# Weight blocks of the feed-forward projections as whole tiles loaded one set ahead, sums written in place

## The chip, the core and the metric

The kernel runs on one core of a Trainium2 chip. The metric is the device time of one execution in microseconds (us). The engines are TensorE (PE; PEld is its weight load), VectorE (DVE), ScalarE (ACT), GpSimd (POOL) and SyncE (SP), whose queue issues most of the transfers.

## The reference, cut to what matters

One encoder layer is computed for 512 + 16 new tokens of one stream and 64 of a running one: attention in two head groups, an output projection, then a gated feed-forward network of width 5632 and a last norm. The change lies in the feed-forward part:

```python
D_MODEL = 2048
D_FF = ((8 * D_MODEL // 3 + 255) // 256) * 256      # 5632
...
    h = rmsnorm(x, lp['norm_ffn_g'])
    x = x + (jax.nn.silu(h @ lp['ffn_w_gate']) * (h @ lp['ffn_w_up'])) @ lp['ffn_w_down']
...
y_prompt = rmsnorm(xp[:, N_META:], final_norm_g)
y_sample = rmsnorm(xs, final_norm_g)
```

All is float32; 576 tokens reach this part (64 and 512).

## The kernel before

**Precision.** A float32 product is made of fp32r products. `split` (L155) makes a high part `wh` on ACT (L156) and the rest `wl` = source - `wh` on DVE (L153). A tile of weights meets the tokens in three matmuls: `wh` with the tokens' high and low parts (L1219), `wl` with the high part (L1223).

**Seven products.** Gate and up take 256 columns at a time, over all 2048 rows. Such a block is seen as eight groups of 2x2 corners of 128x128 (`a11`, `a12`, `a21`, `a22`), and the tokens are cut in two halves of 288, so that seven products of corner sums do for eight (`winograd`, L1154). Left factors by number of the product: 1 is `a11`, 2 is `a12`, 4 is `a22`; 5 is `a21 + a22`, 6 is that less `a11`, 3 is `a12` less the factor of 6, 7 is `a11 - a21`. They run in the order 1, 2, 4, 5, 6, 3, 7 (`WIDE`), in the down projection 1, 5, 6, 2, 7, 3, 4 (`CHAIN`). I call the seven products of one block a set: 7 products of 24 matmuls (16 with `wh`, then 8 with `wl`), 168 in all. There are 44 sets, gate and up in turn (22 pairs, `u` in L1379); the first runs in two halves.

**Factors.** The sums are new tiles `ws`, three buffers (`subtotal`, L1174): 5 and 7 on POOL, 6 and 3 on DVE. `wh` and `wl` have two buffers each, so a product can be split once the one two places earlier is multiplied.

**Raw blocks.** A block is loaded as two halves of 8 K-tiles (1 MB each, L1387). Three buffers of a half take turns, two in the pool `fr`, one in `rw`. A buffer is free when the sums that read it (on POOL and DVE) and the splits are done.

**After a set.** `combined` (L1287) takes the products out of PSUM: copies on ACT (1, 4, 5, 6; L1296) and additions on DVE (2, 3 and twice 7; L1299). `gated` (L1355) multiplies gate by the norm on DVE, applies Silu on ACT, multiplies on POOL (L1360). After the up set POOL multiplies the two (L1420, two halves) and forms four differences of quarters (L1425 to L1428). Then `spill_operands` (L1336) splits the eight quarters: a copy on ACT (L1341), a subtraction on DVE that is written over the quarter (L1342), two stores per four quarters. It is a generator; `step` (L1397) advances it after products, after the fifth in a gate set and after each in an up set. The tiles `c` of gate and up have two buffers each.

**Down.** Five blocks of four such groups and a plain one of two; each block runs over 8 pairs of column tiles `d`, 84 matmuls each (12 a product) in the first five. Its weights come in blocks of 1 MB (`fetch_raw`, two buffers in `fr`), the operands from the spill (`builder`, L1323), the residual `y` from `x2spill` (`load_y`, L1369). The first sum of the first block is made ahead (`total`, L1433). At the end `finish` (L1487) turns the result around on TensorE and writes it out through four buffers `ot`.

**What sets the order.** PE runs as written. The other engines' queues and SP's are filled by a scheduler that follows the program's order but moves instructions up; within its queue each engine runs strictly in order.

Of the kernel before, what the change touches and what calls it, by code (L numbers as in the profile page):

```python
# [11 lines left out]
F32 = mybir.dt.float32  # L12
# [7 lines left out]
P = 128  # L20
D = 2048
KC = D // P
# [93 lines left out]
def encoder_step(  # L116
# [22 lines left out]
    def store(dst, src):  # L139
        nc.sync.dma_start(dst, src)  # L140
# [1012 lines left out]

    def winograd(wpool, spool, raws, slots, take, banks=None, engine=V, step=lambda: None, stag=("ws", 3),  # L1154
                 chain=(), total=None):

# [16 lines left out]

        def subtotal(n, engine, op, xs, ys):  # L1174

            w = spool.tile([P, n, P], F32, name="ws", tag=stag[0], bufs=stag[1])
            k = 0
            for i in range(max(len(xs), len(ys))):
                m = min(x[i].shape[1] for x in (xs, ys) if len(x) > i)
                pick = lambda z: z[i] if len(z) > i and z[i].shape[1] == m else z[0][:, k:k + m, :]  # L1180
                engine.tensor_tensor(w[:, k:k + m, :], pick(xs), pick(ys), op=op)  # L1181
                k += m
            return w
# [4 lines left out]
        sums = {}  # L1188

        def lhs(p):  # L1190
            if p == 5 and total is not None:
                sums[1] = total
                return split_weights(n, [total])
            if p == 6 and total is not None:
                sums[2] = total
                engine.tensor_tensor(total, total, a11[0], op=ALU.subtract)
                return split_weights(n, [total])
            if p in (1, 2, 4):
                return split_weights(n, {1: a11, 2: a12, 4: a22}[p])
# [8 lines left out]
            return split_weights(n, [s])  # L1208

# [37 lines left out]
    for i in range(KC):  # L1247
# [23 lines left out]
        if i == 2:  # L1271
            raw0 = load_raw(rw, w_gate, 0, 8, 0, 1)

    close_mx()
    fr, close_fr = pool("fr")
    fw, close_fw = pool("fw")
    banks0 = {}
# [3 lines left out]
    fb, close_fb = pool("fb", "right")  # L1281

# [53 lines left out]
    def spill_operands(m, parts):  # L1336

        for first, src in parts:
            hi = squad(F32R)
            for k in range(4):  # L1340
                S.activation(hi[:, k], src[:, k], AF.Copy)  # L1341
                V.tensor_tensor(src[:, k].bitcast(F32R), src[:, k], f32(hi[:, k]), op=ALU.subtract)  # L1342
                yield
            store(opspill[m, :, first:first + 4, 0], f32(hi))
            store(opspill[m, :, first:first + 4, 1], src)

    def token_norm():
# [21 lines left out]
    def load_y(d):  # L1369
        if d < 4:  # L1370
            y2 = fc.tile([P, 2, TQ], F32, name="y", tag="c" + "ggu"[d // 2 * 2], bufs=2)
        else:
            y2 = yy.tile([P, 2, TQ], F32, name=f"y{d}")
        for f in range(2):
            y[2 * d + f] = y2[:, f]
            load(y2[:, f], x2spill[2 * d + f])

    start = builder(0, blocks[0], False, True)
    for u in range(FC // 2):  # L1379
        out = {}  # L1380
        for which, wsrc in (("g", w_gate), ("u", w_up)):
            first = turn == 0
            raws = []
            for hf in range(2):
                if turn:
                    rp, bufs = (rw, 1) if turn % 3 == 0 else (fr, 2)
                    raws.append(load_raw(rp, wsrc, hf * 1024, 8, u * 256, bufs))  # L1387
                turn += 1
            c = fc.tile([P, 2, TQ], F32, name="c", tag="c" + which, bufs=2)
            chain = () if first else CHAIN if u == FC // 2 - 1 and which == "u" else WIDE  # L1390
            take = combined(*quarters(c[:, 0, :], c[:, 1, :]), chain)
            if u == FC // 2 - 1 and which == "u":
                raw_down = load_raw(fr, w_down, 0, 2 * blocks[0], 0, 2, start=G.dma_start)
# [15 lines left out]
            if first:  # L1409
                winograd(fw, fb, raws, range(4, 8), take, banks0, step=step)  # L1410
            else:
                winograd(fw, fb, raws, range(8), take, step=step, chain=chain)
            out[which] = c
# [18 lines left out]
        spilling = spill_operands(u, parts)  # L1432
    total = squad()[:, :, 0:P]  # L1433
    corners = raw_down.rearrange("p (m t) (f c) -> p t f m c", t=2, f=2)[:, :, 1]
    G.tensor_tensor(total, corners[:, 0], corners[:, 1], op=ALU.add)
    close_fb()
    close_rw()
    yy, close_yy = pool("yy", "right")

# [20 lines left out]
    def down_rows(m0, n, d, slots, step):  # L1460
# [8 lines left out]
        winograd(fw, yy, raws, slots, take, step=step, chain=CHAIN,  # L1469
                 total=None if m0 + d else total)  # L1470

# [15 lines left out]
    def finish(h, ahead):  # L1487
# [48 lines left out]
    sizes = dict(zip(np.cumsum([0] + blocks).tolist(), blocks))  # L1536
    fetched = {wanted.pop(0): raw_down}

    def fetch_raw():
        if wanted:  # L1540
            key = wanted.pop(0)
            fetched[key] = load_raw(fr, w_down, key[0] * 256, 2 * sizes[key[0]], key[1] * 256, 2)

    for _ in start:
        pass
    first = 0
    for bi, n in enumerate(blocks):
        slots = [(first + k) % 8 for k in range(n)]
        if bi + 1 < len(blocks):
            build = builder(first + n, blocks[bi + 1], bi + 2 == len(blocks))  # L1550

            def step():
                if bi or d:
                    next(spilling, None)
                    next(build, None)

            for d in range(KC // 2):
                fetch_raw()
                if bi == 0 and d + 1 < KC // 2:
                    load_y(d + 1)  # L1560
                down_rows(first, n, d, slots, step)
            for _ in build:
                pass
        else:
            before = iter(())
            for h in range(2):
                for d in range(KC // 2):
                    fetch_raw()
                    plain_rows(first, n, d, (h,), slots, squares)
# [7 lines left out]
    close_yy()  # L1577
    close_fc()
    close_fw()
# [70 lines left out]
```

## Time and profile before

| | |
|---|---|
| median of 3 runs | 2533.42 us (2527.93 to 2533.64) |
| the profiled execution | 2525.37 us, of which the span is 2523.5 us |
| PE busy | 2408.5 us, 95%, 17544 matmuls |
| DVE, ACT, POOL busy | 1851.3, 1138.6 and 822.8 us |
| gate and up sets | 916.57 to 1983.30 us of the span |
| down projection, blocks of four | 1983.30 to 2439.5 us |
| transfers | 271.68 MB read, 81.16 MB written |

Busy time contains the time in which an instruction has begun but waits inside the engine, so a POOL or DVE instruction that stands beside another can be longer than alone. A row of the timeline gives start, length, engine, line, operation and tiles, and in brackets the idle time of the engine before it with what ended it.

### The profile page before, as it was taken

The numbers are of one execution on the slowest core, as the hardware profiler recorded it, in microseconds if no ns is written. First come the engines' busy times: TensorE is split into PE (matmuls) and PEld (weight loads), VectorE is DVE, ScalarE is ACT, GpSimd is POOL, SyncE is SP. The second block draws the span as 40 slices with busy tenths as digits, with TensorE's granted clock in tenths as the row PEclk, the third lists the DMA queues.
The fourth block names the chain that finished last, engine by engine and source line by source line (L and its number), as shares of the span: only waits on it lengthen the run. The fifth ranks groups of instructions, "written<-read, shape, count | busy, mean of one in ns | idle before, by whom it ended". The sixth has DMA issues, their size and how long they took to land. (4 is left out here: it accounts for less than half of the span.)

```text
span 2523.5 us, 44543 instructions
## 1 busy us (share of the span) xinstructions
PE 2408.5 (95%) x17544; PEld 2352.1 (93%) x17544; DVE 1851.3 (73%) x2963; ACT 1138.6 (45%) x2091; POOL 822.8 (33%) x625
## 2 busy tenths in 40 slices
PE   8999999999999999999999999999999999999997
PEld 7999999999998888999998998999999999999997
DVE  5666766577664677777777777777877888898875
ACT  5454544334443444444444444444444433333345
POOL 1100000120001655454455455455455322222236
PEclk9999999999999999999999999999999999999999
DMA  7433233252335543444444435344445874654434
GB/s 225 137 91 89 82 97 90 72 166 86 88 96 158 149 136 105 138 141 139 138 133 148 130 126 160 108 138 141 140 138 164 295 268 157 228 179 137 137 94 151
DMA packets 362742, 353.06 MB, mean 140 GB/s; under 512 B 25086, under 2 KB 320660, under 8 KB 362532
## 3 DMA queue, kind: packets, MB, share of 16 engines
q1 hardware_dynamic: 360575, 344.48, 43.1%
q0 software_dynamic: 1632, 5.19, 0.7%
q8 instruction: 138, 2.26, 0.4%
q10 hardware_dynamic: 325, 0.53, 0.1%
q14 instruction: 72, 0.59, 0.1%
HBM read 271.68 MB, written 81.16 MB: 140 GB/s over the span
## 5 line engine op out<-in xcount | busy, mean ns | idle before, releaser
L1219 PE MATMUL m<-b,wh 128*128 128x288 f32 x7168 | 1054.5, 296 | 3.4 <-ACT wh L156 3.3
L1219 PEld LDWEIGHTS m<-b,wh 128*128 128x128 f32 x7168 | 990.2, 190 | 6.5 <-ACT wh L156 5.2
L1223 PE MATMUL m<-b,wl 128*128 128x288 f32 x3584 | 593.7, 301 | 54.4 <-DVE wl L153 52.6
L1181 POOL TENSOR_TENSOR ws<-raw 128x512 f32<-128x512 f32 x255 | 417.7, 1650 | 584.8 <-DVE wl L153 252.4
L1223 PEld LDWEIGHTS m<-b,wl 128*128 128x128 f32 x3584 | 515.7, 190 | 71.9 <-DVE wl L153 69.4
L156 ACT ACTIVATE wh<-ws 128x512 fp32r<-128x512 f32 (+1 forms) x338 | 286.8, 849 | 351.9 <-PE m L1219 187.3
L153 DVE TENSOR_TENSOR wl<-raw,wh 128x512 fp32r<-128x512 f32 x416 | 407.7, 996 | 21.4 <-ACT wh L156 20.9
L153 DVE TENSOR_TENSOR wl<-ws,wh 128x512 fp32r<-128x512 f32 (+1 forms) x338 | 389.9, 1155 | 41.0 <-ACT wh L156 39.3
L156 ACT ACTIVATE wh<-raw 128x512 fp32r<-128x512 f32 x416 | 249.2, 624 | 214.2 <-PE m L1219 167.1
L108 PE MATMUL ps<-xh,wh 128*128 128x296 f32 x992 | 225.7, 309 | 0.0
L108 PE MATMUL ps<-xl,wh 128*128 128x296 f32 x992 | 217.6, 301 | 0.3 <-DVE xl L161 0.3
L108 PE MATMUL ps<-xh,wl 128*128 128x296 f32 x992 | 217.1, 300 | 0.0
L1181 DVE TENSOR_TENSOR ws<-ws,raw 128x512 f32<-128x512 f32 x127 | 92.2, 727 | 166.8 <-POOL ws L1181 163.4
L108 PEld LDWEIGHTS ps<-xh,wh 128*128 128x128 f32 x992 | 161.3, 190 | 3.5 <-issue 0.6
L108 PEld LDWEIGHTS ps<-xl,wh 128*128 128x128 f32 x992 | 162.2, 190 | 1.0 <-DVE xl L161 0.9
L108 PEld LDWEIGHTS ps<-xh,wl 128*128 128x128 f32 x992 | 162.2, 190 | 0.0
L1467 DVE TENSOR_TENSOR y<-y,m 128x288 f32<-128x288 f32 x280 | 125.7, 449 | 41.6 <-PE m L1223 41.5
L153 DVE TENSOR_TENSOR wl<-wr,wh 128x1024 fp32r<-128x1024 f32 (+1 forms) x110 | 121.6, 1106 | 33.1 <-ACT wh L156 31.1
L156 ACT ACTIVATE wh<-wr 128x1024 fp32r<-128x1024 f32 (+1 forms) x110 | 101.6, 927 | 68.2 <-PE ps L108 50.6
L1341 ACT ACTIVATE s<-c 128x288 fp32r<-128x288 f32 x168 | 63.1, 435 | 150.6 <-POOL c L1420 126.0
L1342 DVE TENSOR_TENSOR c<-c,s 128x288 fp32r<-128x288 f32 x168 | 90.3, 584 | 43.6 <-POOL c L1428 29.4
L1360 POOL TENSOR_TENSOR c<-c,rb 128x576 f32<-128x576 f32 x44 | 71.2, 1618 | 155.7 <-ACT c L1359 155.7
(376 smaller groups left out, 3075.6 us busy)
## 6 DMA issues: line engine op xcount, KB each, us to landing
raw<-in_ffn_w_gate SPq DMA_DIRECT2D x44, 1024.0 KB, 5.4
raw<-in_ffn_w_up SPq DMA_DIRECT2D x44, 1024.0 KB, 5.6
b<-opspill SPq DMA_DIRECT2D x148, 288.0 KB, 6.0
raw<-in_ffn_w_down SPq DMA_DIRECT2D x39, 1024.0 KB, 5.7
wr<-in_w_in SPq DMA_DIRECT2D x56, 512.0 KB, 4.1
opspill<-s SPq DMA_DIRECT2D x42, 576.0 KB, 3.2
opspill<-c SPq DMA_DIRECT2D x42, 576.0 KB, 4.8
wr<-in_w_out SPq DMA_DIRECT2D x16, 512.0 KB, 4.3
```

The costliest lines, as they stand in the source:

```text
L108: self.tc.keep_in_program_order(self.pe.matmul(out, lhsT, rhs, start=start, stop=stop))
L153: V.tensor_tensor(lo, src, f32(hi), op=ALU.subtract)
L156: S.activation(hi, src, AF.Copy)
L1181: engine.tensor_tensor(w[:, k:k + m, :], pick(xs), pick(ys), op=op)
L1219: PE.matmul(banks[p], wh[:, k, :], x, start=first and new and k == 0 and x is hi, stop=False, skip_group_check=not new)
L1223: PE.matmul(banks[p], wl[:, k, :], hi, start=False, stop=last and k == n - 1, skip_group_check=not new)
L1341: S.activation(hi[:, k], src[:, k], AF.Copy)
L1342: V.tensor_tensor(src[:, k].bitcast(F32R), src[:, k], f32(hi[:, k]), op=ALU.subtract)
L1360: G.tensor_tensor(g[:, f, :], g[:, f, :], rb2, op=ALU.mult)
L1467: V.tensor_tensor(c, c, banks[p], op=ALU.add)
```

## The change

Gate and up blocks become one tile of 16 K-tiles (2 MB), one buffer in `fr` and one in `fb`, used in turn; the block of the next set is asked for at the start of a set, ahead of its seven products (`load_pair`). A sum or difference has no tile of its own any more but for one `ws` buffer: 5 is put there by POOL, 6 is written over it by DVE, 3 over `a12` by DVE, 7 over `a21` by POOL. Where there were two instructions of 128x512 per sum and per raw split there is one of 128x1024. `step` advances the spills after products two to six in a gate set (and each in an up set); up's `c` has one buffer. In down, the first two weight blocks come in one tile of `fr` by two POOL-issued loads, the others through two buffers in the place of `fb` (`fd`), asked for after a `d` and not before; seven of the residual tiles lie in the place of the raw block; `total` is gone; the last outputs share three buffers and not four.

```diff
+        sums = []
         def lhs(p):
...
             if p == 5:
-                s = sums[1] = subtotal(n, G, ALU.add, a21, a22)
+                w = spool.tile([P, n, P], F32, name="ws", tag=stag[0], bufs=stag[1])
...
+                for x, y, z in zip(sums, a21, a22):
+                    G.tensor_tensor(x, y, z, op=ALU.add)
             elif p == 6:
-                s = sums[2] = subtotal(n, engine, ALU.subtract, [sums[1]], a11)
+                for x, y in zip(sums, a11):
+                    engine.tensor_tensor(x, x, y, op=ALU.subtract)
             elif p == 3:
-                s = subtotal(n, V, ALU.subtract, a12, [sums[2]])
-            else:
-                s = subtotal(n, G, ALU.subtract, a11, a21)
+                for x, y in zip(sums, a12):
+                    V.tensor_tensor(y, y, x, op=ALU.subtract)
+            elif p == 7:
+                for x, y in zip(a11, a21):
+                    G.tensor_tensor(y, x, y, op=ALU.subtract)
...
+    def load_pair(pool, src, c0, first=0):
+        r = pool.tile([P, 16, 256], F32, name="raw", tag="raw", bufs=1)
+        for i in range(2 - first):
+            r0 = (first + i) * 1024
+            load(r[:, 8 * i:8 * i + 8], src[r0:r0 + 1024, c0:c0 + 256].rearrange("(k p) c -> p k c", p=P))
+        return r
...
-            raws = []
-            for hf in range(2):
-                if turn:
-                    rp, bufs = (rw, 1) if turn % 3 == 0 else (fr, 2)
-                    raws.append(load_raw(rp, wsrc, hf * 1024, 8, u * 256, bufs))
-                turn += 1
-            c = fc.tile([P, 2, TQ], F32, name="c", tag="c" + which, bufs=2)
+            now = raw[:, 0:8] if first else raw
+            if turn < FC - 1:
+                raw = load_pair((fr, fb)[(turn + 1) % 2], (w_up, w_gate)[turn % 2], (turn + 1) // 2 * 256)
+            turn += 1
+            c = fc.tile([P, 2, TQ], F32, name="c", tag="c" + which, bufs=1 + (which == "g"))
...
-                if which == "u" or products[0] > 4:
+                if which == "u" or 1 < products[0] < 7:
                     next(spilling, None)
...
-            tag, bufs = ("ws", 3) if i % 4 < 3 else ("ot", 1)
+            tag, bufs = ("ws", 2) if i % 3 < 2 else ("ot", 1)
...
-                fetch_raw()
                 if bi == 0 and d + 1 < KC // 2:
                     load_y(d + 1)
                 down_rows(first, n, d, slots, step)
+                fetch_raw()
```

**SP's queue in one pair of sets, in the middle of gate and up.** Before (the spill stores are L140, the loads L137):

```order
L140 DMA opspill<-s 128x4x288
L140 DMA opspill<-c 128x4x288
L140 DMA opspill<-s 128x4x288
L137 DMA raw<-in_ffn_w_up 128x8x256
L140 DMA opspill<-c 128x4x288
L137 DMA raw<-in_ffn_w_gate 128x8x256 x2
L137 DMA raw<-in_ffn_w_up 128x8x256
```

Now:

```order
L140 DMA opspill<-s 128x4x288
L140 DMA opspill<-c 128x4x288
L140 DMA opspill<-s 128x4x288
L140 DMA opspill<-c 128x4x288
L137 DMA raw<-in_ffn_w_gate 128x8x256 x2
L137 DMA raw<-in_ffn_w_up 128x8x256 x2
```

The second half of up's block stood between the stores of the spills; both halves now stand ahead of them, behind the gate block of the same pair.

**POOL's queue, one pair.** It starts with the first sums after the multiplications of gate by the norm. Before:

```order
L1360 TENSOR_TENSOR c<-c,rb_9346 128x576 x2
L1181 TENSOR_TENSOR ws<-raw 128x512 x4
L1420 TENSOR_TENSOR c<-c 128x576
L1425 TENSOR_TENSOR c<-c 128x288
L1420 TENSOR_TENSOR c<-c 128x576
L1426 TENSOR_TENSOR c<-c 128x288
L1428 TENSOR_TENSOR c<-c 128x288
L1427 TENSOR_TENSOR c<-c 128x288
L1181 TENSOR_TENSOR ws<-raw 128x512 x4
```

Now (L1185 is the sum of product 5, L1194 the difference of product 7; the other lines moved up by three or up by one):

```order
L1357 TENSOR_TENSOR c<-c,rb_9346 128x576 x2
L1185 TENSOR_TENSOR ws<-raw 128x1024
L1194 TENSOR_TENSOR raw<-raw 128x8x128
L1421 TENSOR_TENSOR c<-c 128x576
L1426 TENSOR_TENSOR c<-c 128x288
L1421 TENSOR_TENSOR c<-c 128x576
L1427 TENSOR_TENSOR c<-c 128x288
L1429 TENSOR_TENSOR c<-c 128x288
L1428 TENSOR_TENSOR c<-c 128x288
L1185 TENSOR_TENSOR ws<-raw 128x1024
L1194 TENSOR_TENSOR raw<-raw 128x8x128
```

Four instructions became two of twice the width, at the same two places between the multiplications; the pair ahead of the two multiplications L1421 belongs to the gate set that follows.

**DVE's queue where an up set ends and the next gate set begins.** Before, from the splits of up's last products to that of product 4 of the gate set:

```order
L1181 TENSOR_TENSOR ws<-ws,raw 128x512 x2
L153 TENSOR_TENSOR wl<-ws,wh 128x1024
L1181 TENSOR_TENSOR ws<-raw,ws 128x512 x2
L1299 TENSOR_TENSOR c<-c,m 128x288
L153 TENSOR_TENSOR wl<-raw,wh 128x512 x2
L1342 TENSOR_TENSOR c<-c,s 128x288
L1299 TENSOR_TENSOR c<-c,m 128x288 x2
L153 TENSOR_TENSOR wl<-raw,wh 128x512 x2
L1342 TENSOR_TENSOR c<-c,s 128x288 x3
L153 TENSOR_TENSOR wl<-raw,wh 128x512 x2
```

Now (L1188 and L1191 are the differences of products 6 and 3):

```order
L153 TENSOR_TENSOR wl<-ws,wh 128x1024
L1188 TENSOR_TENSOR ws<-ws,raw 128x1024
L1191 TENSOR_TENSOR raw<-raw,ws 128x8x128
L153 TENSOR_TENSOR wl<-ws,wh 128x1024
L153 TENSOR_TENSOR wl<-raw,wh 128x1024 x2
L1295 TENSOR_TENSOR c<-c,m 128x288
L153 TENSOR_TENSOR wl<-raw,wh 128x1024
L1338 TENSOR_TENSOR c<-c,s 128x288
L1295 TENSOR_TENSOR c<-c,m 128x288 x2
L153 TENSOR_TENSOR wl<-raw,wh 128x1024
L1338 TENSOR_TENSOR c<-c,s 128x288 x3
L153 TENSOR_TENSOR wl<-raw,wh 128x1024
```

Before, the differences L1181 next to the split of product 7 were those of the following set, made from its block ahead of time; now a set's differences stand in the set itself, between the splits of its products 5 and 6, and no following block is touched before the split of product 7.

More of the change, by code (lines that the diff above doesn't have):

```diff
@@ L1152, in pmt, with winograd @@
         return pm.tile([P, 512], F32, name="m", tag="m")
-    def winograd(wpool, spool, raws, slots, take, banks=None, engine=V, step=lambda: None, stag=("ws", 3),
-                 chain=(), total=None):
+    def winograd(wpool, spool, raws, slots, take, banks=None, engine=V, step=lambda: None, stag=("ws", 1),
+                 chain=()):
         first, last = not banks, take is not None
@@ L1172, in split_weights @@
             return wh, wl
[L1174 to L1183, printed above, removed]
         vs = [r.rearrange("p (m t) (f c) -> p t f m c", t=2, f=2) for r in raws]
@@ L1187, in winograd @@
         a11, a12, a21, a22 = ([v[:, t, f] for v in vs] for f in range(2) for t in range(2))
-        sums = {}
+        sums = []
         def lhs(p):
[L1191 to L1199, printed above, removed]
-            if p == 5:
-                s = sums[1] = subtotal(n, G, ALU.add, a21, a22)
+            if p == 5:
+                w = spool.tile([P, n, P], F32, name="ws", tag=stag[0], bufs=stag[1])
+                ends = np.cumsum([0] + [x.shape[1] for x in a21]).tolist()
+                sums.extend(w[:, a:b, :] for a, b in zip(ends, ends[1:]))
+                for x, y, z in zip(sums, a21, a22):
+                    G.tensor_tensor(x, y, z, op=ALU.add)
             elif p == 6:
-                s = sums[2] = subtotal(n, engine, ALU.subtract, [sums[1]], a11)
+                for x, y in zip(sums, a11):
+                    engine.tensor_tensor(x, x, y, op=ALU.subtract)
             elif p == 3:
-                s = subtotal(n, V, ALU.subtract, a12, [sums[2]])
-            else:
-                s = subtotal(n, G, ALU.subtract, a11, a21)
-            return split_weights(n, [s])
+                for x, y in zip(sums, a12):
[3 more added lines that the diff above has]
+                    G.tensor_tensor(y, x, y, op=ALU.subtract)
+            return split_weights(n, {1: a11, 2: a12, 4: a22, 5: sums, 6: sums, 3: a12, 7: a21}[p])
         shared = {}
@@ L1369, in load_y @@
     def load_y(d):
[L1370 to L1376, printed above, removed]
+        if d < 3:
+            y2 = fc.tile([P, 2, TQ], F32, name="y", tag="cu" if d == 2 else "cg", bufs=1 + (d < 2))
+            y[2 * d], y[2 * d + 1] = y2[:, 0], y2[:, 1]
+        elif d == 3:
+            y7 = fr.tile([P, 7, TQ], F32, name="y7", tag="raw", bufs=1)
+            y.update((6 + i, y7[:, i]) for i in range(7))
+        if d == 6:
+            y.update((i, yy.tile([P, TQ], F32, name=f"y{i}")) for i in range(13, KC))
+        for i in (2 * d, 2 * d + 1):
+            load(y[i], x2spill[i])
     start = builder(0, blocks[0], False, True)
@@ L1392, in encoder_step @@
             if u == FC // 2 - 1 and which == "u":
-                raw_down = load_raw(fr, w_down, 0, 2 * blocks[0], 0, 2, start=G.dma_start)
+                raw = fr.tile([P, 16, 256], F32, name="raw", tag="raw", bufs=1)
+                fetched = {(0, d): raw[:, 8 * d:8 * d + 8] for d in range(2)}
+                for d in range(2):
+                    G.dma_start(fetched[0, d], w_down[0:1024, d * 256:d * 256 + 256].rearrange("(k p) c -> p k c", p=P))
             products = [0]
@@ L1409, in encoder_step @@
             if first:
-                winograd(fw, fb, raws, range(4, 8), take, banks0, step=step)
+                winograd(fw, rw, [now], range(4, 8), take, banks0, step=step)
             else:
-                winograd(fw, fb, raws, range(8), take, step=step, chain=chain)
+                winograd(fw, rw, [now], range(8), take, step=step, chain=chain)
             out[which] = c
@@ L1467, in take @@
                 V.tensor_tensor(c, c, banks[p], op=ALU.add)
-        winograd(fw, yy, raws, slots, take, step=step, chain=CHAIN,
-                 total=None if m0 + d else total)
+        spool, bufs = (yy, 2) if m0 + d else (rw, 1)
+        winograd(fw, spool, raws, slots, take, step=step, stag=("ws", bufs), chain=CHAIN)
     tok = [[(0, NS), (NS, P), (192, 96)], [(QH, P), (416, P), (544, 32)]]
@@ L1561, in encoder_step @@
                 down_rows(first, n, d, slots, step)
+                fetch_raw()
+                if bi + d == 0:
+                    for _ in spilling:
+                        pass
+                    close_rw()
+                    yy, close_yy = pool("yy", "right")
             for _ in build:
@@ L1577, in encoder_step @@
     close_yy()
+    close_fd()
     close_fc()
```

20 lines of the change are left out of this document (9 added, 11 removed).

## The prediction

> **What bounds the kernel now.** First the page, then its stretches by window, because an average over the span hides which stage waits.
>
> ```profile
> span 2523.5 us, 44543 instructions
> PE 2408.5 (95%) x17544; PEld 2352.1 (93%) x17544; DVE 1851.3 (73%) x2963; ACT 1138.6 (45%) x2091; POOL 822.8 (33%) x625
> ```
>
> The next rows are windows: the first four gate and up sets, the 38 that follow, the last two, then the down blocks; last a stretch in which TensorE never waits. The columns are the length, then busy time and count of PE, PEld, DVE, ACT and POOL, and the granted clock.
>
> ```profile
> 916.57:1020.91 104.34, 96.17 (x677) 93.45 (x678) 84.81 (x106) 47.44 (x81) 51.32 (x34) 0.97 0.37 117
> 1020.91:1937.96 917.05, 871.82 (x6385) 860.24 (x6384) 692.84 (x875) 416.63 (x722) 470.96 (x304) 0.99 0.42 137
> 1937.96:1983.30 45.34, 45.27 (x339) 44.80 (x337) 34.41 (x41) 20.35 (x33) 22.27 (x14) 1.00 0.69 229
> 1983.30:2440.00 456.70, 453.10 (x3366) 447.44 (x3365) 398.75 (x644) 178.72 (x285) 106.25 (x79) 1.00 0.55 186
> 1150.00:1200.00 50.00, 49.92 (x375) 49.69 (x375) 40.53 (x50) 24.45 (x41) 24.23 (x18) 1.00 0.40 132
> ```
>
> The last row gives the floor: 50 us for 375 matmuls, 0.1333 us each, 22.4 us for a set of 168. The 38 sets hold 6384 matmuls, 851.2 us at that rate, and take 917.05: 65.9 us are lost, 3.5 per pair (48.27 for a floor of 44.8). The first four sets lose 14.7 of 104.34 us. The down row has 456.70 us for 3366 matmuls, 448.8 at the floor, so little is to be had there. PE busy at 95% says nothing of this: the loss is in the gate and up stage.
>
> What ends TensorE's waits in the 38 sets, from the groups by shape in that window:
>
> ```profile
> L1223 PE MATMUL m<-b,wl 128*128 128x288 f32 x2129 | 338.7, 301 | 45.2 <-DVE wl L153 45.0
> ```
>
> So 45 of the 65.9 us are waits for the low part of a split. Most of the rest is the clock after them: here one wait of 3.15 us, and the 16 matmuls after it take 3.81 us where the next 16 take 2.29.
>
> ```profile
> 1045.50 1.33 PE L1223 MATMUL m<-b,wl 128*128 128x288 f32 x8 [3.15 <-DVE wl L153]
> 1046.68 3.81 PE L1219 MATMUL m<-b,wh 128*128 128x288 f32 x16
> 1050.33 1.22 PE L1223 MATMUL m<-b,wl 128*128 128x288 f32 x8
> 1051.39 2.29 PE L1219 MATMUL m<-b,wh 128*128 128x288 f32 x16
> ```
>
> The timeline of one gate set (1310.1 to 1336.3) shows two waits. The longer one, at its last product:
>
> ```profile
> 1321.65 7.18 POOL L1181 TENSOR_TENSOR ws<-raw 128x512 f32<-128x512 f32 x3 [3.84 <-DVE wl L153]
> 1325.35 0.37 SPq L137 DMA_DIRECT2D raw<-in_ffn_w_up  x1
> 1331.93 1.27 POOL L1181 TENSOR_TENSOR ws<-raw 128x512 f32<-128x512 f32 x1 [3.10 <-DMA raw<-in_ffn_w_up]
> 1333.23 0.69 DVE L1181 TENSOR_TENSOR ws<-ws,raw 128x512 f32<-128x512 f32 x1 [3.68 <-POOL ws L1181]
> 1333.84 1.22 DVE L153 TENSOR_TENSOR wl<-ws,wh 128x1024 fp32r<-128x1024 f32 x1
> 1335.12 1.33 PE L1223 MATMUL m<-b,wl 128*128 128x288 f32 x8 [2.48 <-DVE wl L153]
> ```
>
> Read backwards: the split of product 7 stands in DVE's queue behind a difference of the next set; that waits for POOL's sum, that for the second half of up's block, and that was issued only at 1325.35, when POOL's sum had freed the third buffer. The shorter wait, at product 4 of the set:
>
> ```profile
> 1307.20 1.29 DVE L1181 TENSOR_TENSOR ws<-raw,ws 128x512 f32<-128x512 f32 x2
> 1308.41 0.45 DVE L1299 TENSOR_TENSOR c<-c,m 128x288 f32<-128x288 f32 x1
> 1308.99 1.76 POOL L1420 TENSOR_TENSOR c<-c 128x576 f32<-128x576 f32 x1 [3.69 <-issue]
> 1312.00 0.46 DVE L1342 TENSOR_TENSOR c<-c,s 128x288 fp32r<-128x288 f32 x1 [0.70 <-POOL c L1425]
> 1313.10 2.51 DVE L153 TENSOR_TENSOR wl<-raw,wh 128x512 fp32r<-128x512 f32 x2
> 1313.27 1.80 POOL L1420 TENSOR_TENSOR c<-c 128x576 f32<-128x576 f32 x1 [1.30 <-DVE c L1299]
> 1317.02 0.79 POOL L1427 TENSOR_TENSOR c<-c 128x288 f32<-128x288 f32 x1
> 1317.09 1.78 DVE L1342 TENSOR_TENSOR c<-c,s 128x288 fp32r<-128x288 f32 x3 [1.47 <-POOL c L1428]
> 1318.79 1.28 DVE L153 TENSOR_TENSOR wl<-raw,wh 128x512 fp32r<-128x512 f32 x2
> 1319.52 1.41 PE L1223 MATMUL m<-b,wl 128*128 128x288 f32 x8 [0.69 <-DVE wl L153]
> ```
>
> Here no transfer is late. DVE's spill subtractions wait for POOL's four differences, those for POOL's multiplications of the set before, those for DVE's additions; the split of product 4 stands behind the subtractions.
>
> **The change part by part.** The blocks first. Durations alone and beside the other engine, minimum, median and maximum in ns:
>
> ```profile
> L153 DVE TENSOR_TENSOR wl<-raw,wh x229: 675/683/1930, 1019.1 to 1937.1; 128x512 fp32r<-128x512 f32 x115
> L153 DVE TENSOR_TENSOR wl<-ws,wh x152: 1204/1218/2300, 1030.1 to 1933.7; 128x1024 fp32r<-128x1024 f32 x152
> L1181 POOL TENSOR_TENSOR ws<-raw x152: 1263/1298/3692, 1031.4 to 1931.8; 128x512 f32<-128x512 f32 x152
> ```
>
> A block's load now waits for the split of product 7 two sets earlier. That split can run once product 6 has been multiplied, which is two products (6.4 us) ahead of the end of its set, so the load is out about a full set (22.4 us) before its first split. Two 1 MB loads, one after the other, land in about twice the 6.5 us of the row at 1325.35 (to 1331.9), 13 us: over 9 us to spare. SP's queue has the two loads ahead of the stores, and the stores of a gate set follow within it. DVE has no difference of the next set ahead of the split of product 7 any more. So the longer wait goes, about 2.5 us per pair, and with it the half-speed stretches, worth some 20.9 us (65.9 less 45) over the 38 sets.
>
> The shorter wait stays. For it: the addition of product 3 no longer stands behind two differences (1.29 us at 1307.20), so POOL may begin up to 1.2 us sooner; but three splits on the way are now whole (1.22) and not half (0.68) when the next step follows, 0.54 us each, 1.6 in all. Net 0.4 us later: I take 1.1 us a pair instead of 0.7. Its bounds: 0 if all of the 1.2 us counts and the half splits were never waited for, 2.3 if the 1.6 comes on top of 0.7.
>
> One buffer for the sums: product 5's sum for the next set waits until product 6 of the present one is split. That is two products before the set's end, and the next product 5 begins three products after it, so POOL has about 16 us for 2 x 2.6 us (twice 1.30). Nothing on TensorE's path, if POOL gets its turn. Writing 6 over 5 makes it wait for the splits of 5, which DVE does before it anyway. The spills keep their places in the queues (the shown rows of DVE: one subtraction, then three), so the copies are where they were; up's single `c` has a whole set between the store and the next copy into it. Those edits I cost at nothing; the cover is that of the sums and the store, and a late store would cost ACT's splits behind it what the store is late by.
>
> So a pair is 44.8 + 1.1 = 45.9 us, 19 pairs 872.1: 45 us less (0 to 2.3 us a pair: 66 to 22 less). In the first four sets I give half of the 14.7 back, 7.4 us (0 to 14.7), since the operands of the first set are still late. The last two sets have nothing to give.
>
> Down: the same matmuls, and per `d` the same splits and sums. POOL's two sums of a `d` now follow each other. Where one stands beside a split now:
>
> ```profile
> 2205.45 1.30 POOL L1181 TENSOR_TENSOR ws<-raw 128x512 f32<-128x512 f32 x1 [6.34 <-DMA raw<-in_ffn_w_down]
> 2205.68 1.61 DVE L153 TENSOR_TENSOR wl<-ws,wh 128x512 fp32r<-128x512 f32 x1
> ```
>
> The split takes 0.93 us longer than its 0.68. Two in a row can cost what is left of DVE's lead, or nothing, since a difference (0.69) left the same place: 0, bounds -6 us (the loss of 456.70 over 448.8, most of it) and +8 (0.2 us in each of 40 `d`). The loads asked for after a `d` wait for the same buffer as before.
>
> The end: twelve outputs through four buffers, in rounds that wait for the stores:
>
> ```profile
> 2512.02 1.26 ACT L1521 ACTIVATE ot<-m,rc 128x512 f32<-128x512 f32 x2 [0.67 <-issue]
> 2514.92 0.69 ACT L1521 ACTIVATE ot<-m,rc 128x512 f32<-128x512 f32 x1 [1.64 <-DMA out<-ot]
> 2517.77 0.68 ACT L1521 ACTIVATE ot<-m,rc 32x512 f32<-32x512 f32 x1 [0.72 <-DMA out<-ot]
> ```
>
> A round takes 2.9 us (2512.02, 2514.92, 2517.77). Three buffers make four rounds of the three: 2.9 us more.
>
> Sum: 2525.4 - 45 - 7.4 + 0 + 2.9 = 2475.9 us for an execution like the profiled one. That one lies 8 us under the median of the three runs (2533.4), so the forecast is 2484 us. Its own range, with the bounds above taken half together: 2460 to 2508.
>
> A rule that speaks against the change: VectorE's splits and POOL's sums shut each other out. In the rows above a split of 0.68 us reaches 1.93, and the one at 2205.68 ends 0.54 us after POOL's end. The Trainium skill, "SBUF — State Buffer", section "Who interferes with whom", says that an instruction of VectorE with two SBUF inputs and one of GpSimd that reads SBUF take one shared port, the later one blocked for the whole of the other. By that rule the double-width sums hold VectorE out twice as long, and the sum would be that of the first rival; the trace agrees with the blocking, and no row shows a double-width sum.
>
> **The rivals.** *Longer holds.* A POOL sum of 1024 takes 2.6 us, so a split that meets it waits up to 2.6 us and not 1.3. There are four of them a pair; if one falls on the way to a product, 1.3 us a pair come on: 47.2 us, 19 pairs 20 us less, 2501 us by the profiled execution, 2509 us. For it: DVE and POOL busy add to 1163.8 us in the 917.05 us, so they are rarely both idle. Against: with 1.3 us the up sets ran at the floor, and splits have most of two products' time.
>
> *The sums come late (slower).* In an up set POOL must do sum and difference of the next gate set before the multiplication L1421, in order. If DVE keeps the port, as at 1321.65, where the first of the three sums took 3.7 us (to 1325.35) though 1.3 alone, both slip behind the addition of product 3, and the chain to product 4 starts 2 x 2.6 = 5.2 us later: the wait is 6.3 us and the pair 51.1: 19 x 2.8 = 54 us more, 2575 us, 2583 by the median. It turns slower from about 2.4 us of slip per pair. Against: DVE waits at products 3 and 7 for TensorE, and leaves gaps there.
>
> *The blocks come no earlier.* If SP is held by a store so that the loads go out late, the waits stay: 2533 us. Against it: the order, and the 9 us to spare.
>
> **How the numbers follow.** The forecast gets 0.62, longer holds 0.20, late sums 0.12, no earlier blocks 0.06. The range has to hold the first two: 2460 to 2520 us. Within 0.3% (7.6 us), which is what a measurement of this kernel can tell from no change, lies only the last: 0.06. Faster 0.82, slower 0.12.
>
> **What would show it.** In the windows of the 38 sets: 872 us, clock 1.00, splits ended by no transfer. Right on the loads: no "DMA raw" among the releasers of ACT and POOL there. Right on the shorter wait: TensorE waits for `wl` once a pair, about 1 us, at product 4. Longer holds would show as many splits over 2.3 us that TensorE waits for; late sums as POOL's L1421 beginning after product 7, and gate sets of 28 us. The end would show rounds of three. A pair over 48.3 us makes the prediction wrong.

## The result, and the profile after

The changed kernel takes 2491.26 us (median of 5, 2487.27 to 2493.60) where the kernel before takes 2533.42: a ratio of 0.9836, 95% interval 0.9819 to 0.9854. The forecast was 2484. The profiled execution takes 2493.6 us, 31.8 less than the one of before (2525.4). Two single executions below, 8917 us of kernel 9 and 3837 us of the kernel before beside it, were slow ones and are left out of the medians and ratios.

The first lines of the page after:

```profile
span 2491.8 us, 44116 instructions
PE 2397.9 (96%) x17544; PEld 2343.5 (94%) x17544; DVE 1850.1 (74%) x2748; ACT 1127.2 (45%) x1962; POOL 834.8 (33%) x540
```

The same stretches by window as before, cut at the first matmul of the same sets (columns as there; a set begins with its first matmul):

```profile
919.72:1019.57 99.85, 94.11 (x677) 91.92 (x678) 81.07 (x87) 45.91 (x70) 51.98 (x26) 0.98 0.36 119
1019.57:1885.53 865.96, 854.99 (x6387) 850.17 (x6386) 691.22 (x684) 407.83 (x609) 468.09 (x228) 1.00 0.44 145
1885.53:1930.35 44.82, 44.82 (x338) 44.73 (x337) 32.81 (x34) 19.75 (x29) 18.21 (x10) 1.00 0.76 263
1930.35:2403.89 473.54, 459.35 (x3364) 449.01 (x3363) 407.13 (x645) 178.46 (x285) 123.86 (x79) 1.00 0.53 177
```

The 38 sets go from 917.05 to 865.96 us, 51.1 less (45 forecast): 34 us less of waits, and 17 us less of TensorE's busy time (871.8 to 855.0 us) at a granted clock of 1.00 for 0.99. Down goes from 456.70 to 473.54, some 17 us more, where I had put nothing. The first four sets give 4.5 back (7.4 forecast). After down the kernel needs 87.9 us and before 83.7, 4.2 more (2.9 forecast). Ahead of the sets, where the change touches only how the first block is loaded, the execution after is 3.1 us longer (919.72 for 916.57) at the same PE busy time (875.6 and 875.5 us). The other kernels of this case start the sets anywhere from 917.9 to 923.0, those with the old code there up to 919.8, so this can't be told from chance.

What ends TensorE's waits in the 38 sets now:

```profile
L1210 PE MATMUL m<-b,wl 128*128 128x288 f32 x2130 | 331.0, 297 | 11.0 <-DVE wl L153 11.0
```

45 us of waits for `wl` have become 11. They stand at product 4 of each gate set, the shorter wait that the prediction let stand (one gate set waits at product 3 too). No load of a raw block is any more among what ACT or POOL waits for there. The timeline there (set from 1337.73):

```profile
1335.34 2.35 POOL L1421 TENSOR_TENSOR c<-c 128x576 f32<-128x576 f32 x1 [2.23 <-DVE c L1295]
1338.60 0.46 DVE L1338 TENSOR_TENSOR c<-c,s 128x288 fp32r<-128x288 f32 x1 [2.21 <-POOL c L1426]
1339.87 2.35 POOL L1421 TENSOR_TENSOR c<-c 128x576 f32<-128x576 f32 x1 [1.30 <-DVE c L1295]
1343.91 1.79 DVE L1338 TENSOR_TENSOR c<-c,s 128x288 fp32r<-128x288 f32 x3 [2.99 <-POOL c L1429]
1345.62 1.21 DVE L153 TENSOR_TENSOR wl<-raw,wh 128x1024 fp32r<-128x1024 f32 x1
1346.89 1.34 PE L1210 MATMUL m<-b,wl 128*128 128x288 f32 x8 [0.48 <-DVE wl L153]
```

Read it upwards: the split of product 4 stands behind three spill subtractions, those wait for POOL's differences, and those for the multiplications (L1421). In the first row POOL is idle for 2.23 us ahead of the first multiplication and is released by DVE's addition, not by its own sums: the sums come in time, with that much to spare. All up sets take 22.35 us, the floor, and all but one gate set 23.05 to 23.11 us. The one that does not (25.46) comes up again with kernel 7.

In down the new loss stands at products 2 and 7 of a `d` (on average 2.03 and 1.76 us for 1.59). One `d`, which begins at 2071.62:

```profile
2075.26 1.29 POOL L1185 TENSOR_TENSOR ws<-raw 128x512 f32<-128x512 f32 x1 [8.07 <-ACT wh L156]
2075.38 1.72 DVE L153 TENSOR_TENSOR wl<-raw,wh 128x512 fp32r<-128x512 f32 x1
2076.63 1.61 POOL L1194 TENSOR_TENSOR raw<-raw 128x512 f32<-128x512 f32 x1
2077.13 1.66 DVE L1191 TENSOR_TENSOR raw<-raw,ws 128x512 f32<-128x512 f32 x1
2078.72 0.44 DVE L1464 TENSOR_TENSOR y<-y,m 128x288 f32<-128x288 f32 x1
2079.30 1.30 PE L1206 MATMUL m<-b,wh 128*128 128x288 f32 x8 [1.15 <-DVE y L1464]
```

POOL's sum (L1185) and difference (L1194) follow each other at once. DVE's split and its difference (0.68 and 0.69 alone) take 1.72 and 1.66, one held by each of the two, and the matmuls wait 1.15 us for the addition behind them. Not every `d` loses; that comes up again with kernel 5.

At the end the outputs come in rounds of three, as the sum had it, each 2.5 to 3.8 us after the one before:

```profile
2477.82 1.40 DVE L1520 TENSOR_SCALAR ot<-m,rc 128x512 f32<-128x512 f32 x2
2481.45 0.75 DVE L1520 TENSOR_SCALAR ot<-m,rc 128x512 f32<-128x512 f32 x1 [2.24 <-DMA out<-ot]
2483.94 0.75 DVE L1520 TENSOR_SCALAR ot<-m,rc 128x512 f32<-128x512 f32 x1 [1.74 <-DMA out<-ot]
2487.72 0.75 DVE L1520 TENSOR_SCALAR ot<-m,rc 128x512 f32<-128x512 f32 x1 [2.08 <-ACT ot L1518]
```

### The profile page after: what moved, and what is told of

The parts are those of the page before. It is cut to its first block, busy times and chain, and to the rows that moved or that the text cites. A ratio compares the mean times of both kernels' runs of the same rounds, so it can differ in the third digit from the quotient of the medians.

```text
span 2491.8 us, 44116 instructions
## 1 busy us (share of the span) xinstructions
PE 2397.9 (96%) x17544; PEld 2343.5 (94%) x17544; DVE 1850.1 (74%) x2748; ACT 1127.2 (45%) x1962; POOL 834.8 (33%) x540
## 5 line engine op out<-in xcount | busy, mean ns | idle before, releaser
L153 DVE TENSOR_TENSOR wl<-raw,wh 128x512 fp32r<-128x512 f32 (+1 forms) x457 | 599.0, 1311 | 60.3 <-ACT wh L156 60.0
L1210 PE MATMUL m<-b,wl 128*128 128x288 f32 x3584 | 584.2, 298 | 11.7 <-DVE wl L153 11.6
L156 ACT ACTIVATE wh<-raw 128x512 fp32r<-128x512 f32 (+1 forms) x457 | 380.1, 832 | 409.9 <-PE m L1206 277.9
L1185 POOL TENSOR_TENSOR ws<-raw 128x1024 f32<-128x1024 f32 (+1 forms) x85 | 199.9, 2352 | 626.2 <-DVE wl L153 316.5
L156 ACT ACTIVATE wh<-ws 128x512 fp32r<-128x512 f32 (+1 forms) x170 | 144.2, 848 | 224.2 <-DVE ws L1188 176.2
L1194 POOL TENSOR_TENSOR raw<-raw 128x1024 f32<-128x1024 f32 (+1 forms) x85 | 206.4, 2428 | 6.6
L153 DVE TENSOR_TENSOR wl<-ws,wh 128x512 fp32r<-128x512 f32 (+1 forms) x170 | 163.8, 964 | 17.8 <-ACT wh L156 17.6
L1464 DVE TENSOR_TENSOR y<-y,m 128x288 f32<-128x288 f32 x280 | 125.9, 450 | 47.2 <-PE m L1210 47.1
L1421 POOL TENSOR_TENSOR c<-c 128x576 f32<-128x576 f32 x44 | 101.1, 2298 | 80.5 <-DVE c L1295 78.8
```

What stands on the lines that cost most here:

```text
L153: V.tensor_tensor(lo, src, f32(hi), op=ALU.subtract)
L156: S.activation(hi, src, AF.Copy)
L1185: G.tensor_tensor(x, y, z, op=ALU.add)
L1194: G.tensor_tensor(y, x, y, op=ALU.subtract)
L1210: PE.matmul(banks[p], wl[:, k, :], hi, start=False, stop=last and k == n - 1, skip_group_check=not new)
L1421: G.tensor_tensor(w[:, f, :], w[:, f, :], g[:, f, :], op=ALU.mult)
```

## The experiments

Theory: the gain comes from blocks that are there a set ahead, together with queues that put nothing of the next set ahead of a split; down loses by two POOL instructions in a row. The rivals: the gain comes from the order in DVE's queue alone, or from the wide instructions and the writing in place; POOL's sums come late; POOL's holds are longer. The kernels below were each timed in rounds against the kernel before (2529 to 2532 us there); the stretches are those of one profiled execution, cut at the first matmul of the sets.

| kernel | median, us | ratio to before, 95% | 38 sets, us | down, us |
|---|---|---|---|---|
| before | 2533.4 | | 917.2 | 456.5 |
| changed | 2491.3 | 0.9836 (0.9819 to 0.9854) | 866.0 | 473.5 |
| 1 order alone | 2530.7 | 1.0008 (0.9996 to 1.0020) | 922.8 | 456.3 |
| 2 order and lead | 2471.5 | 0.9776 (0.9751 to 0.9800) | 865.1 | 458.3 |
| 3 second half late | 2626.7 | 1.0387 (1.0357 to 1.0417) | 986.5 | 476.1 |
| 4 sum made twice | 2564.1 | 1.0146 (1.0121 to 1.0172) | 926.1 | 472.9 |
| 5 down, own tile | 2475.4 | 0.9788 (0.9766 to 0.9810) | 867.5 | 455.8 |
| 6 down, sums on DVE | 2489.1 | 0.9846 (0.9819 to 0.9873) | 867.7 | 466.9 |
| 7 product on DVE | 2507.2 | 0.9909 (0.9883 to 0.9936) | 878.8 | 474.8 |
| 8 kernel 2, product on DVE | 2453.3 | 0.9698 (0.9677 to 0.9719) | 849.4 | 457.2 |
| 9 kernel 7 in halves | 2467.4 | 0.9755 (0.9736 to 0.9775) | 849.4 | 466.4 |
| 10 kernel 7, own tiles | 2452.6 | 0.9694 (0.9677 to 0.9712) | 849.4 | 452.8 |

**1 and 2: order, and order with lead.** Both start from the kernel before. The first has two sum buffers for three, in gate and up:

```diff
-winograd(fw, fb, raws, range(8), take, step=step, chain=chain)
+winograd(fw, fb, raws, range(8), take, step=step, chain=chain, stag=("ws", 2))
```

> The kernel before with two sum buffers instead of three in gate and up, nothing else: DVE's difference of product 6 for the next set can no longer stand ahead of the split of product 7, while the block still has three half buffers and up's second half is still asked for in the middle of the gate set. If the place in DVE's queue is what makes the long wait (2.5 us a pair), it goes: the 38 sets take 870 to 885 us where before took 917, the whole 2485 to 2505 us, and TensorE waits at product 7 no more. If the late transfer itself is the cause, the wait moves to the first products of the up set, the 38 sets stay at 905 to 925 us and the whole at 2520 to 2540.

The second has that too, and a fourth half buffer, with one buffer for up's `c` to make room:

```diff
-rp, bufs = (rw, 1) if turn % 3 == 0 else (fr, 2)
+rp, bufs = ((rw, 1), (fr, 2), (fr, 2), (fb, 1))[turn % 4]
-c = fc.tile([P, 2, TQ], F32, name="c", tag="c" + which, bufs=2)
+c = fc.tile([P, 2, TQ], F32, name="c", tag="c" + which, bufs=1 + (which == "g"))
```

> The kernel before with two sum buffers, four half buffers and one buffer for up's c: sums still have tiles of their own, raw splits and sums stay 512 wide, nothing is written over the blocks. If order and lead are all that the change brings, the 38 sets take what they take in the changed kernel, 866 us, and the whole 2475 to 2490, since down is as before. If the wide instructions or the writing in place bring part of it, the sets stay above 880.

The 38 sets of the first, and the half block that up waits for in it (the up set begins at 1335.03):

```profile
1021.60:1944.36 922.76, 883.52 (x6387) 860.97 (x6385) 658.46 (x875) 411.03 (x722) 439.50 (x305) 0.99 0.42 136
...
1329.11 0.37 SPq L137 DMA_DIRECT2D raw<-in_ffn_w_up  x1
1335.56 0.63 ACT L156 ACTIVATE wh<-raw 128x512 fp32r<-128x512 f32 x1 [3.32 <-DMA raw<-in_ffn_w_up]
1338.64 0.79 PE L1223 MATMUL m<-b,wl 128*128 128x288 f32 x4 [1.07 <-DVE wl L153]
```

The wait at product 7 is gone (5.42 us on average before, 3.27 now) and stands at products 1 and 2 of up (5.31 and 3.79 for 3.19). With two sum buffers POOL makes the sums later, so the third half buffer comes free later too: up's second half goes out 17.0 us into the gate set and not 15.3. The order in DVE's queue alone is worth nothing here; the late block finds another place to be waited for. With the fourth half buffer:

```profile
1019.37:1884.49 865.12, 857.79 (x6386) 851.12 (x6385) 685.58 (x875) 407.68 (x722) 478.16 (x305) 1.00 0.45 145
1929.20:2387.47 458.27, 453.84 (x3364) 448.74 (x3363) 396.94 (x643) 178.59 (x285) 104.39 (x79) 1.00 0.55 185
```

865.1 us with 512-wide instructions and sums in tiles of their own, 866.0 in the changed kernel: neither the width nor the writing in place brings anything in itself; they only make the room for the blocks. And since this kernel has down and the four outputs as before (84.0 us from down to the end), it is 20 us faster than the changed one. What the lead alone does, with three sum buffers, was not tried: there is no room for it.

**3: the lead taken back.** In the changed kernel the second half of a block has to follow a one-column copy that ACT makes after product 5 of the set before:

```diff
+if late and products[0] == 4:
+    r_, src_, c0_ = late.pop()
+    S.activation(r_[:, 8, 0:1], cc[:, 1, 575:576], AF.Copy)
+    load(r_[:, 8:16], src_[1024:2048, c0_:c0_ + 256].rearrange("(k p) c -> p k c", p=P))
```

> The changed kernel with the second half of each block held back until product 5 of the set before has been copied out (a one-column copy by ACT into the half, which the load has to follow; that column is overwritten by the load): asked for about 13.5 us into a set, landed at about 20 of 22.4. If only the queue's order matters, the time stays at 2491 within 6 us. If the lead of a full set is needed, waits of 1 to 2.5 us come back in each of 38 sets: 2530 to 2590 us.

It costs 135 us over the changed kernel, more than either theory had. One gate set that begins at 1385.34:

```profile
1383.56 2.41 POOL L1185 TENSOR_TENSOR ws<-raw 128x1024 f32<-128x1024 f32 x1 [11.47 <-DMA raw<-in_ffn_w_gate]
1386.05 3.25 POOL L1194 TENSOR_TENSOR raw<-raw 128x1024 f32<-128x1024 f32 x1
1389.26 1.39 POOL L1433 TENSOR_TENSOR c<-c 128x576 f32<-128x576 f32 x1
1390.68 0.78 ACT L1337 ACTIVATE s<-c 128x288 fp32r<-128x288 f32 x2 [6.11 <-POOL c L1433]
1392.45 4.21 PE L1206 MATMUL m<-b,wh 128*128 128x288 f32 x16 [3.75 <-ACT wh L156]
```

The half lands 1.8 us ahead of its set, in time for the splits. But POOL's sum and difference of this block stand in its queue ahead of the multiplication of the pair before (L1433 here), and both have to wait for the block. The multiplication comes 3.9 us after the set's start and not 2.4 us ahead of it; ACT's spill copies wait for it, and the split of product 2 stands behind them. That is the mechanism of the rival "the sums come late", brought on by a late block. Gate sets take 28.66 us on average, up sets, whose sums nothing so urgent follows, 23.27.

**4: the sum made twice.** POOL makes the sum of product 5 two times over in gate and up:

```diff
-G.tensor_tensor(x, y, z, op=ALU.add)
+for _ in range(1 + (n == 8)):
+    G.tensor_tensor(x, y, z, op=ALU.add)
```

> The changed kernel with POOL's sum of product 5 made twice in gate and up: 2.6 us more on POOL in each set, 5.2 a pair. As I reckoned, POOL has 16 us for 5.2 and now needs 7.8, so only the longer hold of the port shows: 0 to 1.3 us a pair, 2491 to 2516 us. If POOL's sums stand on the path to product 4 (late sums), the multiplications L1421 slip by 2.6 us or more a pair and it takes 2540 us or longer.

A gate set that begins at 1364.41:

```profile
1356.01 6.79 POOL L1186 TENSOR_TENSOR ws<-raw 128x1024 f32<-128x1024 f32 x2 [4.86 <-DVE wl L153]
1362.88 3.27 POOL L1195 TENSOR_TENSOR raw<-raw 128x1024 f32<-128x1024 f32 x1
1366.11 1.43 POOL L1422 TENSOR_TENSOR c<-c 128x576 f32<-128x576 f32 x1
```

POOL's two steps take 6.79 and 3.27 us, 10.1 in all, where the changed kernel has 2.40 and 3.25 at the same place: 4.4 us longer. 2.2 of that were POOL's idle time in the changed kernel. The multiplication starts 1.7 us after the set's start instead of 2.4 us ahead of it, 4.1 us later: 2.2 us by the longer steps, and 1.9 us because they begin later themselves, behind a split of DVE that has slipped too. The gate sets take 26.22 us on average for 23.22, 3.0 more. So the sums do stand on the path, and my 16 us of room for them were no room: what follows them in POOL's queue leaves 2.2.

**5 and 6: down.** In the fifth, product 7's difference of down gets a tile of its own from the same two buffers (from the second `d` on):

```diff
+elif p == 7 and own:
+    w = spool.tile([P, n, P], F32, name="ws", tag=stag[0], bufs=stag[1])
+    G.tensor_tensor(w, a11[0], a21[0], op=ALU.subtract)
+    return split_weights(n, [w])
-winograd(fw, spool, raws, slots, take, step=step, stag=("ws", bufs), chain=CHAIN)
+winograd(fw, spool, raws, slots, take, step=step, stag=("ws", bufs), chain=CHAIN, own=bufs > 1)
```

> The changed kernel with product 7's difference in down in a ws tile of its own (two buffers, as many as there are now), so that it waits for the split of product 7 of the d before and no longer follows the sum of product 5 at once. If the two POOL instructions in a row are what costs down 17 us, the 40 d take 455 to 460 us where the changed kernel took 473.5, the whole 2473 to 2480. If the sum of DVE's and POOL's work on the port decides, wherever it stands, down stays at 470 to 476 and the whole at 2488 to 2494.

In the sixth, DVE makes the sum and the difference of down in place of POOL:

```diff
-G.tensor_tensor(x, y, z, op=ALU.add)
+adder.tensor_tensor(x, y, z, op=ALU.add)
-G.tensor_tensor(y, x, y, op=ALU.subtract)
+adder.tensor_tensor(y, x, y, op=ALU.subtract)
-winograd(fw, spool, raws, slots, take, step=step, stag=("ws", bufs), chain=CHAIN)
+winograd(fw, spool, raws, slots, take, step=step, stag=("ws", bufs), chain=CHAIN, adder=V)
```

> The changed kernel with the sums of products 5 and 7 of down on DVE and none on POOL: DVE per d then has seven splits (0.68), two differences (0.69), seven additions (0.45) and two sums (0.69), 10.7 us of 11.15, and nothing of POOL to wait for. If POOL's holds are the cost, down comes to its floor, 446 to 455 us, the whole 2464 to 2473. If DVE has no 1.4 us to give, or stands behind a block that has not landed, down takes 470 us or more and the whole 2488 or longer.

The fifth, one `d`:

```profile
2074.06 1.29 POOL L1185 TENSOR_TENSOR ws<-raw 128x512 f32<-128x512 f32 x1 [8.12 <-DVE raw L1191]
2074.21 1.69 DVE L153 TENSOR_TENSOR wl<-ws,wh 128x512 fp32r<-128x512 f32 x1
2075.83 0.44 DVE L1468 TENSOR_TENSOR y<-y,m 128x288 f32<-128x288 f32 x1
2075.98 1.30 POOL L1194 TENSOR_TENSOR ws<-raw 128x512 f32<-128x512 f32 x1 [0.63 <-DVE wl L153]
```

Its new tile makes the difference wait for a split of DVE, 0.63 us in which DVE gets on. It does a second thing: the sum now waits for DVE's difference (L1191, first row), and so starts 5.3 to 5.4 us into every `d` but one. The holds are as many and as long, but down takes 455.8 us, 17.7 less (1.2 of it in the first `d`, which the edit leaves alone).

Which of the two it is can be read from the changed kernel, where the pair starts anywhere from 3.6 to 5.6 us into a `d`, always two in a row. The 29 `d` in which it starts 4.39 us in or earlier take 11.70 to 12.64 us; the 8 in which it starts at 4.49 or later take 11.15 to 11.21, the floor. One of the eight, which begins at 2048.66 and takes 11.15:

```profile
2053.77 1.30 POOL L1185 TENSOR_TENSOR ws<-raw 128x512 f32<-128x512 f32 x1 [8.24 <-ACT wh L156]
2055.14 1.63 POOL L1194 TENSOR_TENSOR raw<-raw 128x512 f32<-128x512 f32 x1
```

In the fifth kernel too two `d` have sum and difference in a row, begun 5.4 and 5.9 us in, and take 11.16. So in these traces two in a row cost only where they start early. Early alone does not seem to cost either: in kernel 2 four `d` with a sum by itself at 4.1 to 4.4 us take 11.15. The edit of kernel 5 changes both at once; no run has two apart at the early place in otherwise the same code.

In the sixth, DVE has no holds, but down takes 466.9 and not 455 at most. DVE now stands itself behind a block that has not landed:

```profile
2110.51 0.69 DVE L1185 TENSOR_TENSOR ws<-raw 128x512 f32<-128x512 f32 x1 [0.52 <-DMA raw<-in_ffn_w_down]
```

That row is one `d`. Such waits, of 0.2 to 1.5 us, stand in 30 of the 40 `d`, and these take 11.77 us on average; of the other ten, eight take 11.15 to 11.47. So most of what is left goes with the late blocks; how much is DVE's own load is not shown.

**7 to 10: the chain to product 4.** The multiplications of gate and up go from POOL to DVE, in the changed kernel (7) and in kernel 2 (8):

```diff
-G.tensor_tensor(w[:, f, :], w[:, f, :], g[:, f, :], op=ALU.mult)
+V.tensor_tensor(w[:, f, :], w[:, f, :], g[:, f, :], op=ALU.mult)
```

> The changed kernel with the two multiplications of gate and up (L1421) on DVE, 0.75 us each, not on POOL, 2.35 each: the chain to the split of product 4 loses 3 us and POOL's sums no longer stand ahead of the multiplication. If that chain is what is left of the wait at product 4 (0.76 us a gate set), it goes: the 38 sets take 850 to 856 us where they took 866, the whole 2475 to 2482. If the wait is DVE's own load, 1.5 us a pair more make it 866 to 880 and the whole 2490 to 2505.

> The same edit on the kernel with two sum buffers and four half buffers (2471.5 us, 38 sets in 865.1). By the chain: 850 to 856 us for the sets and 2456 to 2462 for the whole; by DVE's load: 2470 to 2485.

Kernel 8 does what the chain says: every one of its 38 sets takes 22.35 us.

```profile
1018.08:1867.50 849.42, 849.42 (x6386) 849.42 (x6385) 723.59 (x914) 414.74 (x724) 375.46 (x266) 1.00 0.46 148
```

In kernel 7 the wait at product 4 goes too (3.95 to 3.19 us), but one of 1.6 us takes its place at product 3:

```profile
1314.49 5.61 DVE L1338 TENSOR_TENSOR c<-c,s 128x288 fp32r<-128x288 f32 x3
1314.65 2.56 POOL L1185 TENSOR_TENSOR ws<-raw 128x1024 f32<-128x1024 f32 x1 [6.53 <-DVE wl L153]
1317.29 2.49 POOL L1194 TENSOR_TENSOR raw<-raw 128x1024 f32<-128x1024 f32 x1
1320.02 2.35 DVE L153 TENSOR_TENSOR wl<-raw,wh 128x1024 fp32r<-128x1024 f32 x2
1321.29 1.34 PE L1210 MATMUL m<-b,wl 128*128 128x288 f32 x8 [1.30 <-DVE wl L153]
```

Three subtractions of 0.46 us take 5.61, since two of them are held by a whole POOL instruction each. The Trainium skill, "SBUF — State Buffer", section "Who interferes with whom", has the later one blocked for the whole of the other; these rows agree, and show what it comes to when POOL has two in a row. The changed kernel has the same thing once, in the gate set of 25.46 us, which begins at 1383.19:

```profile
1397.94 3.02 DVE L1338 TENSOR_TENSOR c<-c,s 128x288 fp32r<-128x288 f32 x2
1398.10 2.55 POOL L1185 TENSOR_TENSOR ws<-raw 128x1024 f32<-128x1024 f32 x1 [7.99 <-DVE wl L153]
1400.88 4.53 DVE L153 TENSOR_TENSOR wl<-raw,wh 128x1024 fp32r<-128x1024 f32 x2
1404.34 1.33 PE L1210 MATMUL m<-b,wl 128*128 128x288 f32 x8 [1.94 <-DVE wl L153]
```

In its other 18 gate sets the sum begins at the same place, 14.8 us in, and does not get in: it takes 4.05 us for 2.40, and DVE's subtractions and the split behind them run first. The set from 1337.73:

```profile
1352.56 4.05 POOL L1185 TENSOR_TENSOR ws<-raw 128x1024 f32<-128x1024 f32 x1 [7.91 <-DVE wl L153]
1353.14 1.21 DVE L153 TENSOR_TENSOR wl<-raw,wh 128x1024 fp32r<-128x1024 f32 x1
```

Kernel 9 cuts the instructions of kernel 7 in halves (first new line); kernel 10 leaves them wide and gives product 7's difference a tile of its own, in gate and up (second new line, with the lines of kernel 5) and in down:

```diff
-winograd(fw, rw, [now], range(8), take, step=step, chain=chain)
+winograd(fw, rw, [now[:, 0:8], now[:, 8:16]], range(8), take, step=step, chain=chain)
+winograd(fw, rw, [now], range(8), take, step=step, stag=("ws", 2), chain=chain, own=True)
```

> The changed kernel with the multiplications on DVE (2507 us, 38 sets in 878.8, a wait of 1.6 us at product 3 of each gate set) and with gate and up's sums, differences and raw splits in instructions of 512 again, still written over the block. If the width of POOL's instructions holds DVE too long, DVE gets in between them after 1.3 us: the 38 sets take 850 to 860 us, the whole 2477 to 2488. If it is that POOL's instructions for products 5 and 7 follow each other with nothing between, four of 1.3 hold as long as two of 2.6: 875 us or more, 2500 or longer.

> The changed kernel with the multiplications on DVE and product 7's difference in a tile of its own, one more ws buffer, in gate and up and in down; instructions stay 1024 wide (the first half block is loaded in two pieces to make room). The difference then waits for the split of product 7 of the set before, and DVE can work between POOL's two. If the two in a row are what holds DVE: 38 sets in 850 to 856 us, down 455 to 460, the whole 2455 to 2465. If the width does it: the sets stay at 870 or more, the whole at 2480 to 2490.

Both bring the sets to 849.4. In kernel 10 the sum still holds one of the subtractions (2.66 us for 0.46), but the difference comes 3 us later than in kernel 7, and one hold alone does not reach the path. So there it is the two in a row that cost. Kernel 9 gets there another way. A gate set that begins at 1284.28:

```profile
1297.02 1.55 DVE L1338 TENSOR_TENSOR c<-c,s 128x288 fp32r<-128x288 f32 x4
1297.18 5.46 POOL L1185 TENSOR_TENSOR ws<-raw 128x512 f32<-128x512 f32 x2 [7.52 <-DVE wl L153]
1298.50 1.28 DVE L153 TENSOR_TENSOR wl<-raw,wh 128x512 fp32r<-128x512 f32 x2
```

POOL's first sum begins 12.9 us into the set, as in kernel 7, but it does not get in between the subtractions: all four and the two splits behind them run unheld, and the sum takes 3.76 us for 1.3. So kernel 9 does not show that the width costs in itself; it shows a set in which POOL came in later, and why it did is open. Kernels 8 and 10 are the fastest of the case, 38 us below the changed kernel.

## Why the prediction was right, and where it was not

- **The long wait** goes, and the half-speed stretches with it: 51 us less in the 38 sets, for 45 forecast. The reason given was the right one, with its two halves in the wrong balance: the order of DVE's queue without room for the blocks carries nothing, and with it everything (kernels 1 and 2); the room without the order was not run.
- **The shorter wait** stays, at 0.76 us a pair (23.11 less 22.35) and not 1.1. The step that was off is the 1.6 us for whole splits less the 1.2 us for the addition that comes sooner: kernel 2, with half splits, waits 0.83. So the half splits cost no less. 0.3 us over 19 pairs is 6.5 us, and the difference between 45 and 51. That POOL's chain makes this wait is shown by kernels 8 to 10, where it is gone.
- **One sum buffer, the spills.** No wait in the 38 sets is put down to them, as said; the condition for the spills was not run by itself. But the cover that I named for the sums, 16 us, was wrong: 2.2 us (kernel 4).
- **The first four sets** gave 4.5 and not 7.4.
- **Down** is the step that failed: "0, bounds -6 us and +8 (0.2 us in each of 40 `d`)" was +17. The price of one hold had been read rightly (0.93 us), and so had the fact that POOL's two now follow each other; what I did not work out is that then two DVE instructions one after the other are held, and that it matters where. In the 29 `d` in which that starts 4.4 us in or earlier it costs 0.6 to 1.5 us, in the 8 in which it starts later nothing; against before that makes some 14 us. The other 3 us are the first `d` (15.0 us for 12.0): there POOL's last multiplication, a sum and a difference follow each other, and three DVE instructions of 0.69, 0.45 and 0.45 us take 1.80, 1.48 and 1.17. With the multiplications on DVE the first `d` takes 11.15 (kernels 7 to 10). The same code for down takes 476, 473, 475 and 466 us in the kernels 3, 4, 7 and 9, with 7, 9, 6 and 12 `d` in which the pair starts at 4.49 or later.
- **The end** cost 4.2 us for 2.9. Kernel 2, with four buffers, ends as before.
- **The sum**, with before cut at the same matmuls (38 sets 917.2, down 456.5, 83.7 after it): -51.2 - 4.4 - 0.5 + 17.1 + 4.2 + 3.1 is -31.7, the profiled execution's 31.8. That the medians lie 42 us apart is the profiled executions' place: the one of before lay 8 us under its median, this one 2 above. By the stretches the forecast was 18 us too low (49.5 less, where 31.7 came); that it missed the time by 7 only is luck, 10 us of it from where the two profiled executions lay.
- **Rivals.** The blocks did come earlier. The longer holds were priced at 1.3 us a pair in gate and up; there they reached the path once. The argument against them, that the up sets of before ran at the floor, was only about right: those took 22.35 to 23.88 us, 22.7 on average. In down the holds were no longer than before, but two in a row. Kernel 7 shows long ones in every gate set, at 1.6 us. The late sums did not come, but were 2.2 us away; at 4.1 us of slip they cost 3.0 us a pair (kernel 4), so that the sets take 926.1 us and not 917.2. If slip costs one for one once a free part is used up, the free part is 1.1 us, and these sets would be no faster than before from 3.8 us of slip on (1.1 and the 2.7 gained per pair), not from 2.4; that is an estimate from this one slip.

## What to carry to other kernels

In this kernel the order in which the next block's work is queued was worth nothing without room for that block: without it the wait moved to another product; with it, it went, whatever the form of the sums. Before merging instructions or writing results over their sources, look at what the tile of its own did beside holding data: it made POOL's instructions wait for DVE's, and so set where in the `d` they ran, and with what between them. And ask of each queue what stands behind the work that is moved: POOL had 16 us for its sums by the buffers, and 2.2 by the multiplication behind them.

## What the runs showed of the hardware

Where a DVE and a POOL instruction both read two SBUF operands, one is held until the other has ended: in kernel 10 a subtraction of 0.46 us takes 2.66 beside a sum of 2.4. DVE's additions that read one operand from PSUM (L1295 and L1464) are not held: 92 of them in the changed kernel stand beside a POOL instruction, and they take 0.44 to 0.46 us as elsewhere.

When POOL has two instructions in a row, one of DVE gets in between them, and the next one is held for a whole POOL instruction again: in kernel 7 three subtractions of 0.46 us took 5.61 beside two instructions of 2.5. So there DVE lost by how many of its instructions met POOL's, and by POOL's width, not by how much it had to do. The other way round it is not so regular: in 18 of the 19 gate sets of the changed kernel POOL's sum waited for three DVE instructions in a row (4.05 us for 2.40), in the 19th it got in after the first. What decides this the runs do not show.
